# Two parts of a gate's weights loaded into a place of their own, the tied cast reordered, and two parts of a query projection cast early

## The chip, the cores and the metric

One NeuronCore of a Trainium2 chip. The metric is the time of one execution in microseconds (us), the median of several runs. Engines by their short names: PE (TensorE, matmuls), ACT (ScalarE), DVE (VectorE), POOL (GpSimd), SP (SyncE, which here only issues DMAs).

## What is computed

A trunk of two pre-norm layers on 256 tokens of width 1024, float32. Each layer multiplies the normalised input by one wide matrix, splits the result into eleven segments, runs two mixers beside each other (a gated delta rule in both directions, and differential attention), and merges them with two gates:

```python
for l in range(DEPTH):
    h = rmsnorm(x, norm_w[l])
    proj = h @ w_in[l]
    (q_a, k_a, v_a, ab_a, z_a, q_b, k_b, v_b, z_b,
     gate_a, gate_b) = jnp.split(proj, SPLIT_IDX, axis=-1)
    y_a = gated_delta_branch(q_a, k_a, v_a, ab_a, z_a, ...)
    y_b = diff_attention_branch(q_b, k_b, v_b, z_b, ...)
    merged = (sigmoid(gate_a) * (y_a @ w_pa[l])
              + sigmoid(gate_b) * (y_b @ w_pb[l]))
    x = x + merged @ w_out[l]
return rmsnorm(x, final_norm_w)
```

The differential attention has 8 heads, each with two softmaxes over 256 keys whose difference is applied to the values. The delta rule works on chunks of 64 tokens and solves a triangular system for each.

## The kernel before

**Weights in parts.** A projection of 1024 inputs to 1024 outputs is made in two halves of 512 columns, and a half in four parts (kp 0 to 3) of 256 rows. For each part `weights` loads 512 KB (L247, by SP's queue) into a raw tile, casts it to a rounded high part `hi` (L251, on ACT, or on DVE for the parts in `turned`), and takes the rest as a low part, `lo = raw - hi` (L253, on DVE). PE then makes three products of each 128 x 512 block: activation high times hi (L267), high times lo (L268), low times hi (L269); a part is 12 matmuls in `proj_tm`. Raw tiles come from a ring of three ("raw"), hi and lo from rings of two each, so a load can go out when the subtraction that frees its slot is done.

**Homes.** A part can have a home instead of ring tiles for hi and lo: a half of a large tile that is free at the time. Large tiles have tags ("p8" with four buffers, "eo", "ex", "ev", "ktm" and so on), and a new tile of a tag waits for the last reader of the one that had its place. The p8 tiles hold, one after the other, the transposed inputs and the rotated queries and keys of the attention, qkT_0 (heads 0 to 3) and qkT_1 (heads 4 to 7).

**Order of a layer.** The projections follow each other on PE: k and v_b, the first q half, qk (four halves: rotated keys and queries of the attention, named by part and half; qk01 is the second half of the queries), the second q half, v, then zb and za (two halves each), gb, ga (the gates of the attention and of the delta rule), pa and pb, and the output. In layer 0 qk00 starts at 75.8 us, qk01 at 103.4, zb at 163, za at 192, gb at 224.7 and ga at 263. Between them run the decays and the blocks of the triangular solves of the delta rule, on DVE, ACT and POOL, and the attention heads: `scores` (L914, then the maximum L922, the exponentials L924 on ACT, and the combination of the two softmaxes L930 on DVE), `turn` (transposes L941, copy L943) and `attend` (products L952). Head 6's scores come at the end of za's second half, head 7's in gb's first half, and head 7's last products in gb's second half. The solved 32 x 32 blocks are stored to DRAM (udr) and come back in runs of 128 bytes as tiles T (L758, half of them by SP's queue, half by POOL's) and U (L762, POOL's); the products y64p (L776) read T.

**What sets the order.** Each engine runs its instructions in the order of the program, which a list scheduler makes from the source's order, a model of the engines' time, priorities (`high_priority`) and explicit ties (`behind`, which puts an instruction behind another one). Each waits at its place for its inputs. The third and the fourth argument of `gate` give homes to two parts of gb: `wgb` is a pair of p8 tiles, for kp 2 of the first half and kp 1 of the second.

Of the kernel before, what the change touches and what calls it, by code (L numbers as in the profile page):

```python
# [8 lines left out]
F32 = mybir.dt.float32  # L9
F32R = mybir.dt.float32r  # L10
I32 = mybir.dt.int32
AF = mybir.ActivationFunctionType
ALU = mybir.AluOpType
# [4 lines left out]
P = 128  # L18
# [10 lines left out]
HP = None  # L29
# [16 lines left out]
C_QB, C_KB, C_VB, C_ZB, C_GA, C_GB = 4128, 5152, 6176, 7200, 8224, 9248  # L46
# [3 lines left out]
def hybrid_encoder(  # L50
# [18 lines left out]
    nc = tc.nc  # L69
    V, S, G, T = nc.vector, nc.scalar, nc.gpsimd, nc.tensor  # L70
# [6 lines left out]
    wpool = pool("wpool")  # L77
    big = pool("big")
# [25 lines left out]
    mark = {}  # L104
# [116 lines left out]
    def pair(nm):  # L221
        return [big.tile([P, 2, 4, SEQ], F32R, tag="p8", name=f"{nm}_{i}", bufs=4) for i in range(2)]
# [1 line left out]
    def behind(ins):  # L224
        return nullcontext() if ins is None else tc.issue_after(ins)

    def weights(w, c0, n, nm, homes=(None,) * 4, ahead=True, later=None, spare=(), held=None, turned=(), first=()):

        for kp in range(4):
            act, dve = (later or {}).get(kp, (None, None))
            act = mark[nm, act][0] if isinstance(act, int) else act
            with tc.high_priority(offset=HP) if ahead and (homes[kp] is None or kp in first) else nullcontext():
                if homes[kp] is not None:
                    hi, lo = homes[kp] if isinstance(homes[kp], list) else (homes[kp][:, 0], homes[kp][:, 1])
                else:
                    hi = wpool.tile([P, 2, 512], F32R, tag="hi", name=f"hi_{nm}{kp}", bufs=2)
                    lo = wpool.tile([P, 2, 512], F32R, tag="lo", name=f"lo_{nm}{kp}", bufs=2)  # L240
                if kp in spare:
                    raw = work.tile([P, 2, 512], F32, tag="w4a", name=f"raw_{nm}{kp}", bufs=2)
                else:
                    raw = wpool.tile([P, 2, 512], F32, tag="raw", name=f"raw_{nm}{kp}", bufs=3)
                load = (held or {}).get(kp)
                with behind(load):
                    mark["load", nm, kp] = (nc.scalar if load and load.engine != nc.sync.engine else nc.sync).dma_start(  # L247
                        out=raw[:, :, :n],
                        in_=w[kp * 256 : (kp + 1) * 256, c0 : c0 + n].rearrange("(k p) c -> p k c", p=P)).ins
                with behind(act):  # L250
                    high = (V.tensor_copy if kp in turned else S.copy)(hi[:, :, :n], raw[:, :, :n]).ins  # L251
                with behind(dve):
                    mark[nm, kp] = high, V.tensor_tensor(lo[:, :, :n], raw[:, :, :n],  # L253
                                                         hi[:, :, :n].bitcast(F32), ALU.subtract).ins
            for k in range(2):
                yield 2 * kp + k, hi[:, k, :n], lo[:, k, :n]

    def proj_tm(act, w, c0, n, evac, nm, places=(None,) * 4, spare=(), later=None, turned=(), between=None,
                banks=None, held=None, first=()):

        accs = (banks or banks2)(f"pp_{nm}")
        for kt, hi, lo in weights(w, c0, n, nm, places, later=later, spare=spare, turned=turned, held=held,
                                  first=first):
            for m in range(NM):
                ts_ = slice(m * P, (m + 1) * P)
                o = accs[m][:, :n]
                T.matmul(o, act[kt // 4][:, 0, kt % 4, ts_], hi, start=kt == 0, stop=False)  # L267
                T.matmul(o, act[kt // 4][:, 0, kt % 4, ts_], lo, start=False, stop=False)  # L268
                mark["proj"] = T.matmul(o, act[kt // 4][:, 1, kt % 4, ts_], hi, start=False,  # L269
                                        stop=kt == KT - 1).ins  # L270
                mark["done", nm, kt] = mark["proj"]
        if between:
            between()
        for m in range(NM):
            evac(m, accs[m][:, :n])
# [89 lines left out]
    for l in range(DEPTH):  # L365
        lam0 = 0.8 - 0.6 * math.exp(-0.3 * l)
        wl = w_in[l]
# [10 lines left out]
        places = list(homes((("A", 1), ("ktm", 1), ("vtm", 1), ("B", 2)), f"vb{l}"))  # L378
# [4 lines left out]
        later, between, held = {}, None, {}  # L383
# [157 lines left out]
        def conv(seg, c_base, slot, g):  # L541
            def evac_conv(acc, b0):
                vf = []
                for b in range(2):
                    j4 = b0 + b
                    cb = c_base // P + 4 * g + j4
                    ca = work.tile([P, SEQ], F32, tag="conv", name=f"cv{seg}{l}{g}{j4}", bufs=2)
                    S.activation(ca, acc[:, b, :], AF.Copy, scale=cw[:, 2, cb : cb + 1])  # L548
                    for j in (0, 1, 3, 4):
                        sft = j - 2  # L550
                        o0, o1 = max(0, -sft), SEQ - max(0, sft)
                        V.scalar_tensor_tensor(ca[:, o0:o1], acc[:, b, o0 + sft : o1 + sft],  # L552
                                               cw[:, j, cb : cb + 1], ca[:, o0:o1],
                                               ALU.mult, ALU.add)
                    if b == 0:
                        ths = work.tile([P, 2, SEQ], F32, tag="vf", name=f"th{seg}{l}{g}{j4}", bufs=2)
                    th = ths[:, b, :]
                    S.activation(th, ca, AF.Tanh, scale=0.5)
                    if slot is None:
                        f_ = th.rearrange("p (m t) -> p m t", m=NM)  # L560
                    else:
                        f_ = kq[:, 4 * g + j4, :, slot, :]
                    mark["conv"] = V.scalar_tensor_tensor(
                        f_, th.rearrange("p (m t) -> p m t", m=NM), 1.0,
                        ca.rearrange("p (m t) -> p m t", m=NM), ALU.add, ALU.mult).ins
                    vf.append(f_)
                if seg == "q":
                    return
                if seg == "v":
                    tb = squares(f"v{l}{g}{b0}")  # L570
                    turn_squares(tb, ths.rearrange("p b (m t) -> p (b m) t", m=NM))
                    bounce(tb, f"v{l}{g}{b0}")
                    loose.append((tb, 4 * g + b0))
                    return
                pt = bank_c(f"ct{seg}{l}{g}{b0}")
                ptv = pt.rearrange("p (b m d) -> p b m d", b=2, m=NM)
                for b in range(2):
                    for m in range(NM):
                        T.transpose(ptv[:, b, m, :], vf[b][:, m, :], ident)
                bs = slice(4 * g + b0, 4 * g + b0 + 2)  # L580
                S.copy(ktm[:, :, bs, :].rearrange("p m b d -> p b m d"), ptv)
                for b in range(2):
                    for m in range(NM):
                        hd = 4 * g + b0 + b
                        S.activation(sqj[:, :P], ptv[:, b, m, :], AF.Square,
                                     accum_out=ssk[:, m, hd : hd + 1])
            proj_fm(hT, wl, c_base + 512 * g, evac_conv, f"{seg}{l}{g}",
                    turned=(3,) if (seg, g) == ("q", 1) else ())
# [391 lines left out]
            pass  # L980
        log_decays()
        conv("q", C_QA, 1, 0)
        qk_part(0, 0)
        decays(0, 0)
        weigh_k(0, 0)
# [55 lines left out]
                                                   zv[:, j, :], ALU.mult, ALU.mult)  # L1041
                    split_T(yT[i], ov, m, f"{nm}{i}", w=nw_)

        def gate(c_base, nm, tag, between=(None, None), places=((None,) * 4,) * 2, first=()):
            gt = []
            for i in range(2):
                def evac_g(m, ps, i=i):
                    if not gt:
                        gt.extend(e4(nm, tag))
                    S.activation(gt[i][:, m, :], ps, AF.Tanh, scale=0.5)  # L1050
                proj_tm(hT, wl, c_base + 512 * i, 512, evac_g, f"{nm}{i}", places[i], between=between[i],
                        first=first)
            return gt

        def branch(yT, w_, gt, nm, places=(None,) * 4):
            for i in range(2):
# [2 lines left out]
                    V.scalar_tensor_tensor(gs, gs, 1.0, ps, ALU.add, ALU.mult)  # L1059
                proj_tm(yT, w_, 512 * i, 512, evac_p, f"{nm}{i}", (None,) * 4 if i else places)  # L1060

        wgb = [t_.rearrange("p x b t -> p x (b t)").rearrange("p x (k c) -> p x k c", k=2)
               for t_ in pair(f"wgb{l}")]
        gtb = gate(C_GB, f"gb{l}", "ev",
                   (lambda: attend(7, turn(7, es[7], place(34)), place(39)),
                    lambda: [weigh_q(n // 2, n % 2, place((39, 42, 44, 47)[n])) for n in range(4)]),
                   ((None, None, wgb[0], None), (None, wgb[1], None, None)), (1, 2))
        r0 = small.tile([P, NM, NH], F32, tag="r0", name=f"r0{l}")
        V.reciprocal(r0, s_all[:, :, 0, :].rearrange("p h q -> p q h"))
        rb = small.tile([P, NM, NH], F32, tag="rb", name=f"rb{l}")  # L1070
# [126 lines left out]
```

## Time and profile before

| | |
|---|---|
| runs | 768.44, 769.4 and 772.19 us, median 769.4 |
| profiled execution | 770.43 us, span 768.7 us (1.7 us around it) |
| granted clock of PE, mean | 0.996 |
| PE busy | 749.1 us, 97% |
| DVE busy | 577.7 us, 75% |
| ACT busy | 470.8 us, 61% |
| POOL busy | 126.1 us, 16% |
| moved by DMA | 131.24 MB, 171 GB/s |

A row of the timeline gives the start and duration in us, the engine, the line, the operation, what it writes and reads, and in brackets the idle time of the engine before it with what ended it. A row of the windows gives, for a stretch, its length and the busy time (and count) of PE, of PE's weight loads, of DVE, ACT and POOL, then the granted clock of PE, the busy share of the DMA engines and the GB/s. A row of the waits gives the waiting operation, what it waited for, the sum in us, how often, and the longest. Where "x2" stands behind a row, two instructions of a kind came in a row. Durations of PE overlap: a matmul's row runs on after the next has started.

### The profile page before, as it was taken

What the parts mean: (1) busy time and instruction counts of PE and PEld (TensorE: products, weight loads), DVE (VectorE), ACT (ScalarE), POOL (GpSimd) and SP (SyncE); (2) the same over time, 40 slices, a digit from 0 to 9 for tenths busy, and PEclk for the clock granted to TensorE, in tenths of its full rate; (3) what the DMA queues carried; (4) which work ended last, traced back from release to release, by engine and by line L of the source; (5) the groups of instructions that cost most, each with busy time, mean ns of one, the idle gap of its engine ahead of it and who ended that gap; (6) DMA issues with size and microseconds to landing.
All of it is one profiled execution on the core that took longest, in us unless ns stands there. A gap on an engine that the chain in (4) does not pass through costs nothing.

```text
span 768.7 us, 13763 instructions
## 1 busy us (share of the span) xinstructions
PE 749.1 (97%) x5158; PEld 641.8 (83%) x5158; DVE 577.7 (75%) x1083; ACT 470.8 (61%) x1012; POOL 126.1 (16%) x187
## 2 busy tenths in 40 slices
PE   7999999999999999999999999999999889999996
PEld 4899889977877889988889889888787678998884
DVE  5696899999876763478577779999998458437782
ACT  5657675668766574645455668556776557565551
POOL 5100451112031111000010025202111310301000
PEclk9999999999999999999999999999999999999999
DMA  7762767775578242557674257768655934335641
GB/s 230 222 197 60 211 210 210 213 219 171 148 191 202 84 139 86 165 192 239 199 226 140 80 167 245 210 186 232 180 167 160 196 111 133 93 110 192 212 144 55
DMA packets 71795, 131.24 MB, mean 171 GB/s; under 512 B 12288, under 2 KB 12752, under 8 KB 71729
## 3 DMA queue, kind: packets, MB, share of 16 engines
q1 hardware_dynamic: 62718, 111.94, 48.7%
q0 software_dynamic: 6304, 15.15, 7.3%
q10 hardware_dynamic: 2706, 3.28, 1.3%
q8 instruction: 40, 0.66, 0.4%
q14 instruction: 27, 0.21, 0.1%
HBM read 123.44 MB, written 6.91 MB: 170 GB/s over the span
## 4 chain that ended last, share of the span: by engine, by line
PE 72%; DVE 13%; DMA 7%; ACT 4%; issue 3%; POOL 0%; SPq 0%; POOLq 0%; DVEq 0%
PE pp_vb L307 4%; DMA raw_gb<-in_w_in_dram 4%; PE pp_o L307 3%; PE pp_qk L268 2%; PE pp_qk L269 2%; PE pp_qk L267 2%; PE pf_v L323 2%; PE pf_k L327 2%; PE pf_v L327 2%; PE pf_k L325 2%; PE pf_v L325 2%; PE pf_k L323 2%; PE pp_ga L267 2%; PE pp_pb L269 2%; PE pp_ga L269 2%
## 5 line engine op out<-in xcount | busy, mean ns | idle before, releaser
L268 PE MATMUL pp_qk<-lo_qk,hT 128*128 128x512 f32 x128 | 50.9, 398 | 0.2
L269 PE MATMUL pp_qk<-hi_qk,hT 128*128 128x512 f32 x128 | 50.1, 391 | 0.0
L253 DVE TENSOR_TENSOR lo_qk<-raw_qk,hi_qk 128x1024 fp32r<-128x1024 f32 x32 | 40.2, 1257 | 9.7 <-ACT hi_qk L251 9.3
L267 PE MATMUL pp_qk<-hi_qk,hT 128*128 128x512 f32 x128 | 45.2, 393 | 0.0
L251 ACT CAST hi_qk<-raw_qk 128x1024 fp32r<-128x1024 f32 x28 | 29.4, 1050 | 23.5 <-PE pp_qk L269 11.1
L924 ACT ACTIVATE es<-sc,mx 128x256 f32<-128x256 f32 x64 | 29.6, 473 | 17.5 <-DVE mx L922 17.5
L253 DVE TENSOR_TENSOR lo_pb<-raw_pb,hi_pb 128x1024 fp32r<-128x1024 f32 x16 | 19.6, 1225 | 26.8 <-ACT hi_pb L251 26.8
L325 PE MATMUL pf_q<-hT,hi_q 128*128 128x256 f32 x128 | 36.2, 286 | 0.0
L323 PE MATMUL pf_q<-hT,hi_q 128*128 128x256 f32 x128 | 36.1, 287 | 0.0
L323 PE MATMUL pf_v<-hT,hi_v 128*128 128x256 f32 x128 | 35.9, 285 | 0.0
L325 PE MATMUL pf_v<-hT,hi_v 128*128 128x256 f32 x128 | 35.8, 284 | 0.0
L323 PE MATMUL pf_k<-hT,hi_k 128*128 128x256 f32 x128 | 35.7, 284 | 0.0
L325 PE MATMUL pf_k<-hT,hi_k 128*128 128x256 f32 x128 | 35.6, 283 | 0.0
L327 PE MATMUL pf_q<-hT,lo_q 128*128 128x256 f32 x128 | 34.9, 285 | 0.0
L327 PE MATMUL pf_v<-hT,lo_v 128*128 128x256 f32 x128 | 34.5, 288 | 0.0
L327 PE MATMUL pf_k<-hT,lo_k 128*128 128x256 f32 x128 | 34.4, 284 | 0.0
L552 DVE SCALAR_TENSOR_TENSOR cvq<-pf_q,cw,cvq 128x254 f32<-128x254 f32 (+1 forms) x64 | 29.9, 476 | 1.9 <-ACT cvq L548 1.4
L251 ACT CAST hi_pa<-raw_pa 128x1024 fp32r<-128x1024 f32 x16 | 16.9, 1055 | 22.2 <-PE pp_pa L269 16.0
L552 DVE SCALAR_TENSOR_TENSOR cvv<-pf_v,cw,cvv 128x254 f32<-128x254 f32 (+1 forms) x64 | 30.0, 477 | 0.1
L268 PEld LDWEIGHTS pp_qk<-lo_qk,hT 128*128 128x128 f32 x128 | 24.0, 188 | 7.2 <-DVE lo_qk L253 2.3
L552 DVE SCALAR_TENSOR_TENSOR cvk<-pf_k,cw,cvk 128x254 f32<-128x254 f32 (+1 forms) x64 | 28.5, 478 | 2.0 <-ACT cvk L548 1.3
L269 PEld LDWEIGHTS pp_qk<-hi_qk,hT 128*128 128x128 f32 x128 | 24.0, 188 | 4.9
(370 smaller groups left out, 2522.4 us busy)
## 6 DMA issues: line engine op xcount, KB each, us to landing
raw_qk<-in_w_in_dram SPq DMA_DIRECT2D x32, 512.0 KB, 3.8
raw_k<-in_w_in_dram SPq DMA_DIRECT2D x16, 512.0 KB, 4.9
raw_q<-in_w_in_dram SPq DMA_DIRECT2D x16, 512.0 KB, 3.7
raw_v<-in_w_in_dram SPq DMA_DIRECT2D x16, 512.0 KB, 3.8
raw_zb<-in_w_in_dram SPq DMA_DIRECT2D x16, 512.0 KB, 3.7
raw_za<-in_w_in_dram SPq DMA_DIRECT2D x16, 512.0 KB, 3.8
raw_gb<-in_w_in_dram SPq DMA_DIRECT2D x16, 512.0 KB, 5.6
raw_ga<-in_w_in_dram SPq DMA_DIRECT2D x16, 512.0 KB, 4.0
```

What stands on the lines that cost most here:

```text
L251: high = (V.tensor_copy if kp in turned else S.copy)(hi[:, :, :n], raw[:, :, :n]).ins
L253: mark[nm, kp] = high, V.tensor_tensor(lo[:, :, :n], raw[:, :, :n], hi[:, :, :n].bitcast(F32), ALU.subtract).ins
L267: T.matmul(o, act[kt // 4][:, 0, kt % 4, ts_], hi, start=kt == 0, stop=False)
L268: T.matmul(o, act[kt // 4][:, 0, kt % 4, ts_], lo, start=False, stop=False)
L269: mark["proj"] = T.matmul(o, act[kt // 4][:, 1, kt % 4, ts_], hi, start=False, stop=kt == KT - 1).ins
L307: mark["proj"] = T.matmul(o, a_, w_, start=kt == 0 and a_ is ah and w_ is hi, stop=kt == KT - 1 and a_ is al).ins
L323: T.matmul(o, hi[:, cs], act[kt // 4][:, 0, kt % 4, :], start=first, stop=False, skip_group_check=True)
L325: T.matmul(o, hi[:, cs], act[kt // 4][:, 1, kt % 4, :], start=False, stop=False, skip_group_check=True)
L327: T.matmul(o, lo[:, cs], act[kt // 4][:, 0, kt % 4, :], start=False, stop=done, skip_group_check=True)
L552: V.scalar_tensor_tensor(ca[:, o0:o1], acc[:, b, o0 + sft : o1 + sft], cw[:, j, cb : cb + 1], ca[:, o0:o1], ALU.mult, ALU.add)
L924: S.activation(es[:, n, qt, :], spv[:, qt, :], AF.Exp, bias=mx[:, n, qt : qt + 1], accum_out=s_all[:, h, n, qt : qt + 1])
```

## The change

Three edits. First, gb's parts 2 and 3 of the first half are no longer loaded into the ring: one p8 tile, `rgb`, holds the raw weights of both, and their hi and lo come from the rings. Second, only kp 1 of the second half has a home for its hi and lo (`wgb`, now one tile), and its cast is tied behind the cast of kp 0 of that half (`later`). Third, `cast_ahead` loads and casts kp 0 and 1 of qk01 ahead of qk00, with hi and lo in tiles of the tags "eo" and "ex"; `weights` then finds them in `ready`.

```diff
-    def weights(w, c0, n, nm, homes=(None,) * 4, ahead=True, later=None, spare=(), held=None, turned=(), first=()):
+    def weights(w, c0, n, nm, homes=(None,) * 4, ahead=True, later=None, spare=(), held=None, turned=(), first=(), raws={}):
...
         for kp in range(4):
+            if (nm, kp) in ready:
+                hi, lo = ready.pop((nm, kp))
+                for k in range(2):
+                    yield 2 * kp + k, hi[:, k, :n], lo[:, k, :n]
+                continue
...
-                if kp in spare:
+                if kp in raws:
+                    raw = raws[kp]
+                elif kp in spare:
...
+    def cast_ahead(w, c0, nm, kp, tag):
+
+        hi, lo = (big.tile([P, 2, 512], F32R, tag=tag, name=f"{x_}_{nm}{kp}", bufs=2) for x_ in ("ah", "al"))
+        raw = wpool.tile([P, 2, 512], F32, tag="raw", name=f"raw_{nm}{kp}", bufs=3)
+        with tc.high_priority(offset=HP):
+            nc.sync.dma_start(out=raw, in_=w[kp * 256 : (kp + 1) * 256, c0 : c0 + 512].rearrange("(k p) c -> p k c", p=P))
+            high = S.copy(hi, raw).ins
+            mark[nm, kp] = high, V.tensor_tensor(lo, raw, hi.bitcast(F32), ALU.subtract).ins
+        ready[nm, kp] = hi, lo
...
         log_decays()
         conv("q", C_QA, 1, 0)
+        for kp, tag in enumerate(("eo", "ex")):
+            cast_ahead(wl, C_QB + 512, f"qk{l}01", kp, tag)
         qk_part(0, 0)
...
                 proj_tm(hT, wl, c_base + 512 * i, 512, evac_g, f"{nm}{i}", places[i], between=between[i],
-                        first=first)
+                        later={1: (0, None)} if i and places[i][1] is not None else None,
+                        first=first, raws=raws[i])
...
-        wgb = [t_.rearrange("p x b t -> p x (b t)").rearrange("p x (k c) -> p x k c", k=2)
-               for t_ in pair(f"wgb{l}")]
+        rgb = big.tile([P, 2, 2, 512], F32, tag="p8", name=f"rgb{l}", bufs=4)
+        wgb = big.tile([P, 2, 2, 512], F32R, tag="p8", name=f"wgb{l}", bufs=4)
...
-                   ((None, None, wgb[0], None), (None, wgb[1], None, None)), (1, 2))
+                   ((None,) * 4, (None, wgb, None, None)), (1,),
+                   ({2: rgb[:, 0], 3: rgb[:, 1]}, {}))
```

How the order of the engines' programs moves, in layer 0 (layer 1 is alike). A name's number tells apart tiles of one name. SP's queue before, from the last za loads on: raw_gb_2645, 2663, 2679 and 2697 are the four parts of gb's first half, 2736, 2752, 2770 and 2788 those of the second.

```order
L247 DMA raw_za_2498<-in_w_in_dram 128x2x512
L247 DMA raw_za_2516<-in_w_in_dram 128x2x512
L247 DMA raw_gb_2645<-in_w_in_dram 128x2x512
L247 DMA raw_gb_2663<-in_w_in_dram 128x2x512
L247 DMA raw_gb_2679<-in_w_in_dram 128x2x512
L247 DMA raw_gb_2697<-in_w_in_dram 128x2x512
L758 DMA T_2628<-udr_343 32x16x32 x2
L247 DMA raw_gb_2736<-in_w_in_dram 128x2x512
L758 DMA T_2628<-udr_343 32x16x32 x2
L247 DMA raw_gb_2752<-in_w_in_dram 128x2x512
L247 DMA raw_gb_2770<-in_w_in_dram 128x2x512
```

And now, first at the head of za's second half, then from gb's part 0 on (raw_gb_2645 and 2663 stand just ahead of the second piece).

```order
L254 DMA raw_za_2360<-in_w_in_dram 128x2x512
L254 DMA rgb_2639<-in_w_in_dram 128x2x512 x2
L254 DMA raw_za_2462<-in_w_in_dram 128x2x512
...
L254 DMA raw_gb_2736<-in_w_in_dram 128x2x512
L254 DMA raw_gb_2752<-in_w_in_dram 128x2x512
L777 DMA T_2628<-udr_343 32x16x32 x4
L254 DMA raw_gb_2770<-in_w_in_dram 128x2x512
```

The loads of kp 2 and 3 of the first half went to the front, into rgb, and the first two loads of the second half stand ahead of the four T loads instead of among and behind them.

ACT before, from the cast of gb's part 0 to that of the second half's part 0 (es_2543 belongs to head 6, es_2577 to head 7).

```order
L251 CAST hi_gb_2643<-raw_gb_2645 128x1024
L943 COPY aT_2537<-at_2536 128x512
L251 CAST wgb_0_2639<-raw_gb_2679 128x1024
L924 ACTIVATE es_2543,s_all_350<-sc_2546,mx_2544 128x256 x2
...
L251 CAST hi_gb_2695<-raw_gb_2697 128x1024
L943 COPY aT_2571<-at_2570 128x512
L924 ACTIVATE es_2577,s_all_350<-sc_2580,mx_2578 128x256 x2
L924 ACTIVATE es_2577,s_all_350<-sc_2579,mx_2578 128x256 x2
L251 CAST wgb_1_2640<-raw_gb_2752 128x1024
L251 CAST hi_gb_2734<-raw_gb_2736 128x1024
```

And now, in the same stretch (hi_gb_2679 and hi_gb_2696 are cast from rgb).

```order
L962 COPY aT_2537<-at_2536 128x512
L943 ACTIVATE es_2543,s_all_350<-sc_2546,mx_2544 128x256 x2
L943 ACTIVATE es_2543,s_all_350<-sc_2545,mx_2544 128x256 x2
L258 CAST hi_gb_2643<-raw_gb_2645 128x1024
...
L943 ACTIVATE es_2577,s_all_350<-sc_2580,mx_2578 128x256 x2
L943 ACTIVATE es_2577,s_all_350<-sc_2579,mx_2578 128x256 x2
L258 CAST hi_gb_2679<-rgb_2639 128x1024
...
L258 CAST hi_gb_2696<-rgb_2639 128x1024
L962 COPY aT_2714<-at_2713 128x512
L258 CAST hi_gb_2734<-raw_gb_2736 128x1024
L258 CAST wgb_2640<-raw_gb_2752 128x1024
```

The cast into wgb_0 ahead of head 6's exponentials is gone, part 0's cast stands behind them, and the cast into wgb stands behind that of hi_gb_2734.

PE before, at the end of gb's first half.

```order
L268 MATMUL pp_gb_2642<-lo_gb_2696,hT_1_108 128x512
L269 MATMUL pp_gb_2642<-hi_gb_2695,hT_1_108 128x512
L267 MATMUL pp_gb_2732<-hi_gb_2734,hT_0_107 128x512
L267 MATMUL pp_gb_2733<-hi_gb_2734,hT_0_107 128x512
L268 MATMUL pp_gb_2732<-lo_gb_2735,hT_0_107 128x512
L269 MATMUL pp_gb_2732<-hi_gb_2734,hT_0_107 128x512
...
L654 MATMUL kq_2804<-kq_329 128x128
L776 MATMUL y64p_3191<-T_2621,A_339 32x32
L776 MATMUL y64p_3226<-T_2628,A_339 32x32
```

And now, at the same place (y64p comes 64 times between the two pieces).

```order
L288 MATMUL pp_gb_2642<-hi_gb_2696,hT_1_108 128x512
L971 MATMUL av_2720<-vb_1_133,aT_2714 128x128
L673 MATMUL kq_2804<-kq_329 128x128
L971 MATMUL av_2720<-vb_1_133,aT_2714 128x128
L673 MATMUL kq_2804<-kq_329 128x128
...
L795 MATMUL y64p_3226<-T_2628,A_339 32x32
L286 MATMUL pp_gb_2732<-hi_gb_2734,hT_0_107 128x512
```

Head 7's products (av_2720), the first products kq of the decays, and all y64p now stand ahead of gb's second half; before, they stood behind its part 1.

DVE before, where the parts of qk01 are cast (hi_qk_1327 and 1345 are its kp 0 and 1, 1363 its kp 2; kk are products of the decays' blocks).

```order
L680 TENSOR_TENSOR A_339<-kk_1081,dsum_1079 128x512
L251 CAST hi_qk_1327<-raw_qk_1329 128x1024
L253 TENSOR_TENSOR lo_qk_1328<-raw_qk_1329,hi_qk_1327 128x1024
L679 TENSOR_TENSOR dsum_1103<-B_340 128x512
L251 CAST hi_qk_1345<-raw_qk_1347 128x1024
L680 TENSOR_TENSOR A_339<-kk_1105,dsum_1103 128x512
L253 TENSOR_TENSOR lo_qk_1346<-raw_qk_1347,hi_qk_1345 128x1024
L679 TENSOR_TENSOR dsum_1127<-B_340 128x512
```

And now, first among the convolutions of the second k half (cvk), then at the place of before.

```order
L571 SCALAR_TENSOR_TENSOR cvk_656<-pf_k_534,cw_268,cvk_656 128x254
L274 TENSOR_TENSOR al_qk_964<-raw_qk_965,ah_qk_963 128x1024
L582 SCALAR_TENSOR_TENSOR kq_329<-thk_513,cvk_516 128x2x128
...
L571 SCALAR_TENSOR_TENSOR cvk_683<-pf_k_535,cw_268,cvk_683 128x255
L274 TENSOR_TENSOR al_qk_970<-raw_qk_971,ah_qk_969 128x1024
L571 SCALAR_TENSOR_TENSOR cvk_683<-pf_k_535,cw_268,cvk_683 128x254
...
L260 TENSOR_TENSOR lo_q_1273<-raw_q_1274,hi_q_1272 128x1024
L260 TENSOR_TENSOR lo_qk_1364<-raw_qk_1365,hi_qk_1363 128x1024
L698 TENSOR_TENSOR dsum_1091<-B_340 128x512
L699 TENSOR_TENSOR A_339<-kk_1093,dsum_1091 128x512
L698 TENSOR_TENSOR dsum_1115<-B_340 128x512
```

The two casts and two subtractions of kp 0 and 1 are gone from between the blocks; two subtractions (al_qk) stand among the convolutions, and the two casts are on ACT.

More of the change, by code (lines that the diff above doesn't have):

```diff
@@ L256, in weights @@
                 yield 2 * kp + k, hi[:, k, :n], lo[:, k, :n]
+    ready = {}
+    def cast_ahead(w, c0, nm, kp, tag):
[6 more added lines that the diff above has]
+        ready[nm, kp] = hi, lo
     def proj_tm(act, w, c0, n, evac, nm, places=(None,) * 4, spare=(), later=None, turned=(), between=None,
[L259 removed]
+                banks=None, held=None, first=(), raws={}):
         accs = (banks or banks2)(f"pp_{nm}")
         for kt, hi, lo in weights(w, c0, n, nm, places, later=later, spare=spare, turned=turned, held=held,
[L263 removed]
+                                  first=first, raws=raws):
             for m in range(NM):
@@ L1042, in gated, with gate @@
                     split_T(yT[i], ov, m, f"{nm}{i}", w=nw_)
-        def gate(c_base, nm, tag, between=(None, None), places=((None,) * 4,) * 2, first=()):
+        def gate(c_base, nm, tag, between=(None, None), places=((None,) * 4,) * 2, first=(),
+                 raws=({}, {})):
             gt = []
```

## The prediction

> **What bounds the kernel now.** I read the busy shares first, then PE's waits over the whole span, then the 20 us windows in which PE falls short, and last the timeline of each engine in those windows.
>
> ```profile
> PE 749.1 (97%) x5158; PEld 641.8 (83%) x5158; DVE 577.7 (75%) x1083; ACT 470.8 (61%) x1012; POOL 126.1 (16%) x187
> PE at L941 <- DVE es L930: 2.8, 2, 1.6
> PE pp_gb L267 <- ACT hi_gb L251: 2.7, 2, 2.3
> PE pp_gb L268 <- DVE lo_gb L253: 1.4, 2, 0.7
> 220.00:240.00 20.00, 18.41 (x100) 14.52 (x99) 11.14 (x20) 10.80 (x30) 6.90 (x12) 1.00 0.91 228
> 600.00:620.00 20.00, 15.85 (x75) 11.92 (x74) 11.26 (x19) 13.27 (x37) 5.13 (x10) 0.96 0.80 160
> 60.00:200.00 140.00, 139.78 (x856) 121.09 (x855) 127.28 (x262) 95.46 (x217) 31.52 (x47) 1.00 0.64 187
> ```
>
> PE is busy 97% of the span, so only time in which PE stands still, or runs at a lower clock, can be won. Three lines of its waits, 6.9 us in all, belong to one place that comes twice: the projection gb of each layer (about 224 to 248 us and 597 to 624 us). The windows say the same: 18.41 and 15.85 of 20 us there, against 139.78 of 140 between the start and z.
>
> The timeline of PE in layer 1 (start, duration, idle time before in brackets) shows three stops; "x2" is two matmuls in a row.
>
> ```profile
> 600.82 0.39 PE L269 MATMUL pp_gb<-hi_gb,hT 128*128 128x512 f32 x1
> 602.38 0.74 PE L941 MATMUL at<-ident,es 128*128 128x128 f32 x4 [1.17 <-DVE es L930]
> 613.33 0.39 PE L268 MATMUL pp_gb<-lo_gb,hT 128*128 128x512 f32 x1
> 613.55 0.39 PE L269 MATMUL pp_gb<-hi_gb,hT 128*128 128x512 f32 x1
> 616.20 0.73 PE L267 MATMUL pp_gb<-hi_gb,hT 128*128 128x512 f32 x2 [2.26 <-ACT hi_gb L251]
> 617.65 0.50 PE L268 MATMUL pp_gb<-lo_gb,hT 128*128 128x512 f32 x1 [0.72 <-DVE lo_gb L253]
> ```
>
> Matmuls of this shape start 0.22 to 0.23 us apart when nothing stops them (613.33 to 613.55); a stop costs the distance of the starts less 0.23. At 602.38 that is 1.56 - 0.23 = 1.33 us; at 616.20 it is 2.65 - 0.23 = 2.42; the second matmul of the pair starts 0.73 - 0.39 = 0.34 after 616.20, so the stop at 617.65 costs 1.11 - 0.23 = 0.88. Sum 4.6 us. Layer 0 has the same three:
>
> ```profile
> 228.06 0.39 PE L269 MATMUL pp_gb<-hi_gb,hT 128*128 128x512 f32 x1
> 230.04 0.74 PE L941 MATMUL at<-ident,es 128*128 128x128 f32 x4 [1.59 <-DVE es L930]
> 241.21 0.39 PE L269 MATMUL pp_gb<-hi_gb,hT 128*128 128x512 f32 x1
> 241.99 0.73 PE L267 MATMUL pp_gb<-hi_gb,hT 128*128 128x512 f32 x2 [0.40 <-ACT hi_gb L251]
> 243.44 0.50 PE L268 MATMUL pp_gb<-lo_gb,hT 128*128 128x512 f32 x1 [0.72 <-DVE lo_gb L253]
> ```
>
> 1.98 - 0.23 = 1.75, 0.78 - 0.23 = 0.55, and 1.11 - 0.23 = 0.88: 3.2 us. After the long stop of layer 1 the granted clock drops as well:
>
> ```profile
> 618.00:620.00 2.00, 2.00 (x7) 1.61 (x6) 0.78 (x1) 1.69 (x3) 0.00 (x0) 0.63 0.88 302
> 620.00:622.00 2.00, 2.00 (x6) 1.53 (x5) 0.45 (x1) 0.40 (x1) 0.00 (x0) 0.52 0.78 222
> ```
>
> The clock is the last number but two: 0.63 and 0.52 in those 4 us, so 2 x (0.37 + 0.48) = 1.7 us of full-speed work are missing. Together 3.2 + 4.6 + 1.7 = **9.5 us** lie in the two gb stages.
>
> **Why PE stops there.** ACT takes its work in order, and two of its casts wait for a load:
>
> ```profile
> 226.24 1.05 ACT L251 CAST wgb<-raw_gb 128x1024 fp32r<-128x1024 f32 x1 [4.34 <-DMA raw_gb<-in_w_in_dram]
> 239.94 1.05 ACT L251 CAST wgb<-raw_gb 128x1024 fp32r<-128x1024 f32 x1 [3.01 <-DMA raw_gb<-in_w_in_dram]
> 598.58 1.05 ACT L251 CAST wgb<-raw_gb 128x1024 fp32r<-128x1024 f32 x1 [3.92 <-DMA raw_gb<-in_w_in_dram]
> 614.15 1.04 ACT L251 CAST wgb<-raw_gb 128x1024 fp32r<-128x1024 f32 x1 [4.88 <-DMA raw_gb<-in_w_in_dram]
> 615.11 1.04 ACT L251 CAST hi_gb<-raw_gb 128x1024 fp32r<-128x1024 f32 x1
> DMA to landing us min/median/max: 3.6/5.6/9.7
> 220.28 2.79 SPq L247 DMA_DIRECT2D raw_gb<-in_w_in_dram  x2
> 228.58 0.39 SPq L247 DMA_DIRECT2D raw_gb<-in_w_in_dram  x1
> 232.05 10.60 SPq L247 DMA_DIRECT2D raw_gb<-in_w_in_dram  x3
> 604.39 12.46 SPq L247 DMA_DIRECT2D raw_gb<-in_w_in_dram  x3
> ```
>
> The first wgb cast (598.58) stands ahead of the exponentials of head 6; they start when it is done, DVE's es L930 follows, and PE's transposes at L941 wait for that. The second (614.15) waits for a load issued at 604.39 and landed at 614.13, and stands ahead of the cast of the part that PE needs first (615.11): a cast that is needed later holds up one that is needed now.
>
> **The change, part by part.** (1) Parts 2 and 3 of gb's first half are loaded straight into a large tile of their own before z's second half. The two loads that stood at 220.28 are no longer there, and the first two loads of the second half move up into their place, ahead of the T loads: from 228.58 and 232.05 to about 220.3 and 223 (the slots of the ring come free as before). With the longest landing of any gb load, 9.7 us, they are in by 230 and 233, and PE wants the first at about 241. In ACT's order no cast of gb stands ahead of head 6's exponentials any more; the cast into wgb comes after that of part 0 of its half. So both waits on a load go: -1.75 and -1.33 (transposes), -0.55 and -2.42 (hi), -0.88 twice (lo). What is late next on the transposes' path is the chain mx, es, L930; the trace's windows from 60 to 200, where the same heads run with no cast waiting, lose 0.2 us in 140, so it fits. The lower clock follows the longest stop within 2.5 us, and I take it to go with it: -1.7. **Sum -9.5**, bounds 0 (all stops stay) and -9.5.
>
> Beside that place, the Trainium skill, page "TensorE: Matmul & The Clock Gate", section "Why this matters for your kernels", asks for no PE-idle gap over about 3 us, since one idle window halves the clock. Here a gap of 2.65 us with a second of 1.1 us behind it already halved it, and the 1.98 us gap of layer 0 did not; the measurement decides. By the page's figure alone the half clock would have another cause than this gap and would stay, and the sum would be -7.8.
>
> (2) The two loads into the large tile must wait for the last reader of the tile whose room they take, the scores of head 3, and za's second half queues behind them on SP.
>
> ```profile
> 181.68 25.18 SPq L247 DMA_DIRECT2D raw_za<-in_w_in_dram  x8
> 196.85 1.13 PE L914 MATMUL sc<-qkT 64*128 64x256 f32 x8
> ```
>
> In the new order these scores stand ahead of za's first part on PE; now they stand behind a few matmuls of it, and end at 198. The eight za loads go out some 3.5 us apart (25.18 over seven steps), the fifth at about 196. So even at the scores' old place it would go some 2 us later, and no wait of PE for za is among those above 0.2 us: the loads run ahead of need. Cost 0, bounds 0 and 2 a layer.
>
> (3) Two parts of qk's second q projection (kp 0 and 1) are cast early: two loads, two ACT casts and two DVE subtractions a layer move from about 100 us to about 55 to 67 us.
>
> ```profile
> 100.00:120.00 20.00, 19.86 (x119) 16.79 (x118) 19.65 (x33) 12.89 (x31) 9.90 (x14) 1.00 0.73 212
> 60.00:80.00 20.00, 20.00 (x140) 18.67 (x139) 13.62 (x30) 15.07 (x45) 2.93 (x1) 1.00 0.30 82
> L253 DVE TENSOR_TENSOR lo_qk<-raw_qk,hi_qk 128x1024 fp32r<-128x1024 f32 x32 | 40.2, 1257 | 9.7 <-ACT hi_qk L251 9.3
> 100.78 0.68 DVE L251 CAST hi_qk<-raw_qk 128x1024 fp32r<-128x1024 f32 x1
> 101.56 1.61 DVE L253 TENSOR_TENSOR lo_qk<-raw_qk,hi_qk 128x1024 fp32r<-128x1024 f32 x1
> ```
>
> DVE is full at 100 to 120 us (19.65) and has room at 60 to 80 (13.62). It loses 2 x (0.68 + 1.61) = 4.6 us there and takes 2 x 1.26 = 2.5 us on here; ACT takes 2 x 1.05 on, with 5 us free. On the path that sets the end this is worth only PE's idle time of those stretches, 0.14 us in this window and 0.1 in that of layer 1: **-0.3**, bounds 0 and -1.
>
> (4) What these pieces push back. In layer 0 the logarithms of the decays, and what follows from them down to the solves, come behind the new pieces on ACT and DVE: 0 to 2 x (1.05 + 1.26) = 4.6 us later. qk's own first parts are cast on the same two engines right after, and could reach PE late by as much. I take 1 us of new stops in all, near the end at 0, since DVE has 6 us free in 60 to 80: **+1.0**, bounds 0 and 4.6. With the casts out of the way, the order also places head 7's last product and the first solve products (y64p) ahead of gb's second half on PE. These need the T loads:
>
> ```profile
> L758 POOL DMA_DIRECT2D T<-udr x4: 648/648/649, 230.3 to 232.3; - x4
> DMA to landing us min/median/max: 2.2/5.9/7.9
> 235.76 1.05 PE L952 MATMUL av<-vb,aT 128*128 128x128 f32 x8
> ```
>
> The last issue at 232.3 plus the longest landing 7.9 is 240.2; PE comes there at about 241.44 - 1.75 + 1.6 (eight products of head 7 and eight of the solve, some 0.8 us for each eight: 1.05 less the 0.25 by which the last one's duration runs on) = 241.3. Slack 1 us, and two big loads fewer are in flight beside them. Cost 0, with the price in a rival.
>
> **Sum.** The profiled execution took 770.43 us (span 768.7): 770.4 - 9.5 - 0.3 + 1.0 = 761.6. It lies 1.0 over the median of 769.4, so on the median **760.6 us**.
>
> **Rivals.** A difference under 0.5% (3.8 us) can't be told from none.
> - A, as above: 760.6; 758 to 763.5. Chance 0.56.
> - B, the wait moves on: T lands 1 to 3 us later than reckoned, or the solves' inputs are late by (4), and PE, which now meets y64p ahead of a projection part that could have covered it, stands 0 to 2 us in each layer; or the lower clock stays (1.7). For it: DMA was 0.91 busy in 220 to 240. Against: the same issue times and less traffic. 760.6 + 2 to 5 = 763 to 765.5. Chance 0.22.
> - C, the change doesn't do what it says: loads ahead on SP get no earlier, since the ring's slots come free later, behind the casts that now stand behind the exponentials on ACT. Then the hi and lo stops (1.43 and 3.30) and the clock stay, and only the transposes' 3.1 go: 769.4 - 3.1 - 0.3 + 1 = 767. Against: the ring has two users fewer. Chance 0.14.
> - D, slower: y64p's T waits on the whole decay chain of (4), in both layers. A chain 4.6 us later leaves PE 3.6 us at y64p in each, 7.2 in all, which takes the gain to 768; from 6 us later in each layer (5 us of stop, 10 in all, over the 9.8 gained) the kernel is slower, and at 8 us (14 of stop) it takes 773.6. For it: that order puts the decays behind two more casts. Against: the decays are made over 100 us ahead of T's loads, and DVE has idle time on the way to take a delay up. Chance 0.08.
>
> **How the numbers follow.** The likeliest is A. From 757.5 (A with (4) at 0, the 1.0 of (3), and 1 us between runs) to 767.5 (up to C) lie some 8 in 10. Faster by over 0.5% is below 765.6: A and nearly all of B, 0.77. Within: C and a rest of D and B, 0.17. Slower: 0.06.
>
> **What would show it.** Right: no wait of ACT on a gb load, PE's waits at L941 and at the gb matmuls under 0.3 us each, PE at least 19.7 of 20 in 220 to 240 and in the same stretch of layer 1, and the granted clock at 1.00 there. For B and D: a PE wait at y64p on T or U. For C: the casts of gb's second half still waiting for a landing. For (4): waits of PE on lo_qk between 75 and 90 us. Wrong outright: a new stop in ga, pa or pb, whose order I read as hardly changed.

## The result, and the profile after

The changed kernel takes 766.95 us (median of 20 runs, 765.16 to 769.83), the kernel before 769.47 (median of 20). The ratio is 0.9969, with a 95% interval of 0.9954 to 0.9984: 2.4 us faster, by 1.2 to 3.5. The forecast was 760.6, or 8.8 us less than the median of before. The profiled execution took 765.96 us (span 764.3), 4.5 less than that of before; single executions lie up to 4 us from their median, so the medians carry the size, and the profiles the places.

The page of the changed kernel, its busy line:

```profile
PE 746.6 (98%) x5158; PEld 640.3 (84%) x5158; DVE 572.3 (75%) x1079; ACT 475.3 (62%) x1016; POOL 122.7 (16%) x187
```

PE's idle time fell from 19.6 to 17.7 us, 1.9, where 6.9 had been at gb alone. What PE waits for now, without the layers' first projection (operation, releaser, sum in us, times, longest):

```profile
PE wb_n L165 <- POOL tri L116: 3.1, 1, 3.1
PE pp_zb L287 <- DVE lo_zb L260: 2.6, 3, 1.6
PE pf_q L346 <- DVE lo_q L260: 1.4, 2, 0.7
PE at L960 <- DVE es L949: 0.6, 1, 0.6
PE pp_pa L287 <- DVE lo_pa L260: 0.5, 1, 0.5
```

The three gb lines of before are gone altogether; the wait at L960 (L941 before) that is left is one in za. In their place stand lines that the list of before does not have: the low parts of zb, of the first q half (lo_q) and of pa. The windows at gb, in both layers (length, then busy time of PE; the clock is the last number but two):

```profile
220.00:240.00 20.00, 20.00 (x106) 16.20 (x107) 13.99 (x24) 14.05 (x38) 9.28 (x16) 1.00 0.97 211
594.00:614.00 20.00, 20.00 (x109) 16.14 (x108) 13.62 (x22) 15.22 (x39) 7.01 (x13) 1.00 0.80 178
552.00:556.00 4.00, 2.37 (x13) 1.73 (x12) 4.00 (x8) 3.60 (x11) 0.56 (x1) 1.00 0.26 74
```

PE never stops in the first two, and the granted clock is 1.00 in all three. The last row is the new hole: in zb of layer 1, PE stands 1.63 of 4 us.

PE's timeline at the new stops:

```profile
70.80 0.39 PE L346 MATMUL pf_q<-hT,lo_q 128*128 128x256 f32 x1 [0.67 <-DVE lo_q L260]
183.23 0.50 PE L287 MATMUL pp_zb<-lo_zb,hT 128*128 128x512 f32 x1 [0.85 <-DVE lo_zb L260]
554.57 0.50 PE L287 MATMUL pp_zb<-lo_zb,hT 128*128 128x512 f32 x1 [1.63 <-DVE lo_zb L260]
567.01 0.41 PE L960 MATMUL at<-ident,es 128*128 128x128 f32 x2 [0.63 <-DVE es L949]
```

Counted from start to start, as in the prediction, the stops of the trace are: lo_q 0.83 and 0.86, lo_zb 1.02 in layer 0 and 0.33 + 1.79 in layer 1, the transposes 0.79, lo_pa 0.69. Sum 6.3 us, against the 9.5 us (7.8 of stops, 1.7 of lower clock) that left gb. The question for the experiments was which edit brought the 6.3, and by what.

### The profile page after: what moved, and what is told of

Its sections match the earlier page's. It is cut to its first block, busy times and chain, and to the rows that moved or that the text cites. A ratio compares the mean times of both kernels' runs of the same rounds, so it can differ in the third digit from the quotient of the medians.

```text
span 764.3 us, 13758 instructions
## 1 busy us (share of the span) xinstructions
PE 746.6 (98%) x5158; PEld 640.3 (84%) x5158; DVE 572.3 (75%) x1079; ACT 475.3 (62%) x1016; POOL 122.7 (16%) x187
## 5 line engine op out<-in xcount | busy, mean ns | idle before, releaser
L287 PE MATMUL pp_qk<-lo_qk,hT 128*128 128x512 f32 x112 | 43.9, 392 | 0.0
L288 PE MATMUL pp_qk<-hi_qk,hT 128*128 128x512 f32 x112 | 43.7, 390 | 0.0
L260 DVE TENSOR_TENSOR lo_qk<-raw_qk,hi_qk 128x1024 fp32r<-128x1024 f32 x28 | 34.4, 1228 | 9.0 <-ACT hi_qk L258 8.8
L286 PE MATMUL pp_qk<-hi_qk,hT 128*128 128x512 f32 x112 | 39.7, 392 | 0.0
L260 DVE TENSOR_TENSOR lo_pb<-raw_pb,hi_pb 128x1024 fp32r<-128x1024 f32 x16 | 19.6, 1226 | 23.0 <-ACT hi_pb L258 23.0
L260 DVE TENSOR_TENSOR lo_ga<-raw_ga,hi_ga 128x1024 fp32r<-128x1024 f32 x16 | 19.5, 1219 | 20.6 <-ACT hi_ga L258 20.6
L287 PE MATMUL pp_zb<-lo_zb,hT 128*128 128x512 f32 x64 | 26.0, 407 | 2.6 <-DVE lo_zb L260 2.6
```

## The experiments

**Two theories.** O: the gb edit is worth its whole gain, and the two parts cast ahead cost about 6 us by the stops above. G: the gb edit is worth only part, because what fills its stops comes late elsewhere, and the parts cast ahead are harmless. Each run is compared with runs of the kernel before on the same chip.

**1. The gb edit alone.**

```diff
-        for kp, tag in enumerate(("eo", "ex")):
-            cast_ahead(wl, C_QB + 512, f"qk{l}01", kp, tag)
```

> The change without the two parts cast ahead; gb's raw tile and the tied cast stay. Theory O (the two parts cast ahead cost about 6 us by the stops that appear at lo_q, at lo_zb, at the transposes in za and at lo_pa; the gb edit is worth its whole 9.5): 760 us, ratio to before 0.987 to 0.989, no PE wait over 0.3 us between 60 and 224 us. Rival G (the stops of gb are only partly won, since what fills them comes late elsewhere, and the parts cast ahead are harmless): 766 to 767, with stops in z as in the changed kernel.

Measured 761.29 us (ratio 0.9908, 0.9882 to 0.9934), 1.3 above the 760 of theory O and far from G. Of PE's waits, outside the layers' first steps there is left:

```profile
PE pp_pa L287 <- DVE lo_pa L260: 0.5, 1, 0.5
```

No gb, no z, no q line. lo_pa is new against the kernel before, so that stop belongs to the gb edit.

**2. The two parts cast ahead alone**, gb as in the kernel before (homes, order and loads of before, `cast_ahead` kept).

> The kernel before with only the two parts of qk01 cast ahead; gb as before. Theory O: slower, 773 to 776 us (before + 4 to 6.5), with the waits of PE at lo_q (0.8 a layer), at lo_zb (1.0 in layer 0, 2.1 in layer 1) and at the transposes in za, and gb's stops as before. Rival G: 769 to 770, no difference.

Measured 774.81 us (ratio 1.0085, 1.006 to 1.011): 6.7 us slower.

```profile
PE pp_zb L287 <- DVE lo_zb L260: 3.6, 3, 1.9
PE pp_gb L286 <- ACT hi_gb L258: 2.9, 2, 2.6
PE at L960 <- DVE es L949: 2.3, 2, 1.7
PE pf_q L346 <- DVE lo_q L260: 1.8, 2, 1.0
```

Here both families stand together: gb's old stops and the new ones. Runs 1 and 2 decide for O: the gb edit wins 6.9 us and the early parts cost 6.7. The whole change gave -2.4 and the sum of the two is -0.2; each part is uncertain by about 2 us, so it is not shown whether they add.

**3. One part (kp 0) instead of two.** The loop is `enumerate(("eo",))`.

> The change with one part (kp 0) of qk01 cast ahead instead of two. The order of the engines' programs in the stages zb and za is then that of the kernel before again, while the order up to qk01 is changed. Theory O, with the order in z as the cause of the larger half (3.9 of 6.3 us): 760 to 762 us, no stop at lo_zb and at the transposes. If instead the added work itself is the cause (one part is half of it): 763 to 764, with stops in z of half the size. Rival G: 766 to 767.

Measured 759.73 us (0.9885, 0.9862 to 0.9909), with none of the new stops but lo_pa (0.5 again), and one in k of layer 1 (abq) that runs 1 and 2 don't have:

```profile
PE abq L526 <- ACT abT L523: 1.3, 1, 1.3
```

Half of the added work costs none of the 6 us. It is not the amount of work alone, then. In this kernel the order of PE, ACT and DVE in zb and za is that of before, row for row; in the changed kernel it is another one, in both layers, on all three engines.

**4. The same work, the other order.** One part again, but kp 2. That leaves the q halves nearly as before, and gives z, in both layers, the order of the changed kernel's layer 0.

> As the run with one part cast ahead, but kp 2 of qk01 instead of kp 0: the same added work (one load, one ACT cast, one DVE subtraction a layer). The programs' order in the first and second q half is then nearly that of the kernel before, and in zb and za, in both layers, that of layer 0 of the changed kernel. If the order in z is the cause of its stops: a stop of PE at lo_zb of about 1 us in each layer, 761.5 to 763 us. If the amount of work cast ahead is the cause: none, 759.5 to 760.5 us, as with kp 0.

Measured 763.1 us (0.9923, 0.9899 to 0.9948), with stops at lo_zb in both layers (0.66 and 0.86 from start to start) and none at lo_q (besides lo_pa, 0.7 us at abq and 0.2 at lo_qk are left):

```profile
PE pp_zb L287 <- DVE lo_zb L260: 1.2, 2, 0.7
```

**5. Two parts, z's order as before.** kp 1 and 2 in layer 0, kp 0 in layer 1.

> Two parts (kp 1 and 2) of qk01 cast ahead in layer 0, one (kp 0) in layer 1: the order in zb and za is that of the kernel before in both layers, while layer 0's order in the q halves is changed as in the changed kernel. If the order in z is the cause: no stop at lo_zb or at the transposes; a stop at lo_q of up to 0.9 us in layer 0 alone; 759.7 to 761 us. If the work of two parts is the cause: a stop of about 1 us at lo_zb in layer 0 as in the changed kernel, 761.5 to 763 us.

Measured 761.13 us (0.9896, 0.9873 to 0.9919). PE waits for lo_q, once, in the layer with two parts; no wait for lo_zb:

```profile
PE pf_q L346 <- DVE lo_q L260: 0.8, 1, 0.8
```

**6. Two parts in both layers, z's order as before only in layer 0** (kp 1 and 2 there, kp 0 and 1 in layer 1).

> Two parts cast ahead in both layers: kp 1 and 2 in layer 0, where the order in z is that of the kernel before, and kp 0 and 1 in layer 1, where it is that of the changed kernel's layer 1. If the order in z is the cause: no stop in z in layer 0, and in layer 1 the 2.1 us at lo_zb and 0.8 at the transposes; with 0.8 us at lo_q in each layer 763.5 to 765 us. If the work is the cause: stops in z in both layers, 766 to 767 us.

Measured 766.31 us (0.9966, 0.995 to 0.9982). By the time alone this is the 766 to 767 us of the other theory, in which the work is the cause; the profiled execution took 764.87 and was the fastest of the twelve. The places decide, and they are those of the order: lo_q in both layers (1.6 us of waits), lo_zb at 536.87 and 553.10, in layer 1 alone, and the transposes at 565.60. Why the median lies 1.3 us over the 763.5 to 765 expected is open.

Runs 3 to 6 cross work and order: the stops in z follow the order, and the stop at lo_q follows two parts in a layer.

**7. What in the order does it.** ACT in zb of layer 1; first the changed kernel, then the one before:

```profile
548.86 0.70 ACT L618 ACTIVATE vtm<-tb_v,nrm 128x128 f32<-128x128 f32 x2 [1.24 <-DMA tb_v<-bnc_v]
549.46 0.40 ACT L577 ACTIVATE thv<-cvv 128x256 f32<-128x256 f32 x1
549.77 0.68 ACT L618 ACTIVATE vtm<-tb_v,nrm 128x128 f32<-128x128 f32 x2
550.36 0.58 ACT L355 ACTIVATE zb<-pp_zb 128x512 f32<-128x512 f32 x1
550.83 1.04 ACT L258 CAST hi_zb<-raw_zb 128x1024 fp32r<-128x1024 f32 x1
```

```profile
549.43 0.61 ACT L336 ACTIVATE zb<-pp_zb 128x512 f32<-128x512 f32 x1
549.90 1.07 ACT L251 CAST hi_zb<-raw_zb 128x1024 fp32r<-128x1024 f32 x1
550.84 0.63 ACT L336 ACTIVATE zb<-pp_zb 128x512 f32<-128x512 f32 x1
551.33 1.30 ACT L599 ACTIVATE vtm<-tb_v,nrm 128x128 f32<-128x128 f32 x4
```

The copies vtm bring the values of the delta rule back from a turn through DRAM (tb_v). Before, they stood behind the cast of zb's second half, kp 1; now they stand ahead of it, and ACT waits 1.24 us for their DMA. ACT's wait of this kind adds up to

```profile
ACT vtm L618 <- DMA tb_v<-bnc_v: 6.3, 4, 2.8
```

in the changed kernel. Where z has no stops, the list of ACT's waits has no such line (before and run 5), or one of 0.8 and 0.3 us (runs 1 and 3); in runs 2, 4 and 6 it has 9.4, 3.7 and 3.4 us.

How the wait reaches PE is seen on DVE, in the changed kernel (the last row is PE in run 6):

```profile
177.76 0.42 DVE L582 SCALAR_TENSOR_TENSOR thv<-thv,cvv 128x256 f32<-128x256 f32 x1 [1.09 <-ACT thv L577]
181.96 1.21 DVE L260 TENSOR_TENSOR lo_zb<-raw_zb,hi_zb 128x1024 fp32r<-128x1024 f32 x1
549.90 0.42 DVE L582 SCALAR_TENSOR_TENSOR thv<-thv,cvv 128x256 f32<-128x256 f32 x1 [0.46 <-ACT thv L577]
553.30 1.22 DVE L260 TENSOR_TENSOR lo_zb<-raw_zb,hi_zb 128x1024 fp32r<-128x1024 f32 x1
564.73 0.17 DVE L946 RECIPROCAL cc<-s_all 128x2 f32<-128x2 f32 x1 [2.19 <-ACT es L943]
553.10 0.50 PE L287 MATMUL pp_zb<-lo_zb,hT 128*128 128x512 f32 x1 [1.06 <-DVE lo_zb L260]
```

It does not come by the cast: that ends at 551.87, and DVE takes up lo_zb at 553.30. It comes by thv, a step of the convolution that stands behind the first of the copies on ACT, and for which DVE stands idle. In layer 0 DVE loses 1.09 us there and has no gap from there to lo_zb, and PE stops for 1.02. In layer 0 of run 2 and both layers of run 4, with the same order, DVE loses 1.78, 0.70 and 0.90 us there, and PE's stops are 1.71, 0.66 and 0.86: this stop is the wait for tb_v. The transposes hang on it as well, by the exponentials behind the fourth batch of copies (ACT waits 2.75 us for it, DVE 2.19).

In layer 1 it is the smaller part: DVE loses 0.46 us, and PE stops for 1.79. In run 6, with that order in layer 1, DVE loses nothing on the way to lo_zb and PE still stops for 1.22. The rest is the order on DVE itself: between the subtractions of kp 0 and kp 1 DVE works 4.71 us in the kernel before (548.51 to 553.22) and 5.79 in run 6 (546.04 to 551.83). The 0.33 at the first stop has no wait for tb_v ahead of it either. So of the 3.9 us in z, 2.3 (1.02, 0.46 and 0.79) hang on tb_v and 1.7 (0.33 and 1.33) on DVE's order, as worked out from these rows.

To test the wait for tb_v, the copies alone were tied to where they stood, with the rest of the change whole:

```diff
                 place_v(mark[f"zb{l}0", 1][0])
-                place_v(mark[f"zb{l}0", 3][0])
             elif p == 1:
                 place_v(mark[f"zb{l}1", 1][0])
+            elif p == 2:
+                place_v(mark[f"za{l}0", 1][0])
```

> The whole change, with two batches of the copies vtm on ACT tied later: the third behind zb's second half, kp 1, the fourth behind za's first half, kp 1, which is where they stand in the kernel before. The order in the q halves (with its stops at lo_q) and from ga on stays that of the changed kernel. Theory: in the changed kernel these copies came ahead of that cast of zb and ACT stood waiting for their DMA (tb_v), 1.2 to 2.8 us, which made lo_zb and the transposes late. Then the stops at lo_zb (3.1 us in all) and at the transposes (0.8) go and those at lo_q (1.7) stay: 763 to 764 us, ratio to before 0.991 to 0.993. If the stops in z come from DVE's own crowding and not from that wait: 766 to 767.5 us.

Measured 762.7 us (0.9916, 0.9894 to 0.9937). The line on tb_v is gone from ACT's waits; of PE's, past the layers' start:

```profile
PE pf_q L346 <- DVE lo_q L260: 1.7, 2, 0.8
PE pp_pa L287 <- DVE lo_pa L260: 0.5, 1, 0.5
PE pp_zb L287 <- DVE lo_zb L260: 0.3, 2, 0.2
```

The waits for lo_zb fall from 2.6 to 0.3 us, those at the transposes go, and lo_q stays (1.7), at 0.3 us under the time expected. But the tie also put DVE's rows in z in another order than either kernel: the two subtractions of layer 1 are 4.87 us apart (546.61 to 551.48), near the 4.71 of before. So this run takes both causes away at once and does not tell them apart; the rows above do.

**8. The stop at lo_q.** The first q half's kp 2, DVE in the changed kernel:

```profile
64.67 1.23 DVE L274 TENSOR_TENSOR al_qk<-raw_qk,ah_qk 128x1024 fp32r<-128x1024 f32 x1 [0.56 <-ACT ah_qk L273]
65.81 0.48 DVE L571 SCALAR_TENSOR_TENSOR cvk<-pf_k,cw,cvk 128x254 f32<-128x254 f32 x1
66.21 0.41 DVE L582 SCALAR_TENSOR_TENSOR kq<-thk,cvk 128x256 f32<-128x256 f32 x1
67.72 0.43 DVE L582 SCALAR_TENSOR_TENSOR kq<-thk,cvk 128x256 f32<-128x256 f32 x1 [1.10 <-ACT thk L577]
68.09 1.52 DVE L571 SCALAR_TENSOR_TENSOR cvk<-pf_k,cw,cvk 128x254 f32<-128x254 f32 x3
69.53 1.22 DVE L260 TENSOR_TENSOR lo_q<-raw_q,hi_q 128x1024 fp32r<-128x1024 f32 x1
```

lo_q's cast begins at 67.95 on ACT and takes 1.04, so it is ready at 68.99; DVE is still at the three convolution steps of 68.09, which the early part pushed back, and starts 0.54 us later than it could. The early part pushes on two engines: its subtraction takes 1.23 us of DVE, and its cast stands on ACT ahead of its load, and ahead of the thk that DVE waits 1.10 us for:

```profile
63.59 1.05 ACT L273 CAST ah_qk<-raw_qk 128x1024 fp32r<-128x1024 f32 x1 [1.59 <-DMA raw_qk<-in_w_in_dram]
```

To test it, the two subtractions were tied behind those of q's parts 2 and 3:

```diff
+            with behind(mark[f"q{nm[2]}0", 2 + kp][1]):
-            mark[nm, kp] = high, V.tensor_tensor(lo, raw, hi.bitcast(F32), ALU.subtract).ins
+                mark[nm, kp] = high, V.tensor_tensor(lo, raw, hi.bitcast(F32), ALU.subtract).ins
```

> The change, with the two early subtractions tied behind the subtractions of the first q half's parts 2 and 3. The stop at lo_q (0.83 and 0.86) comes from the early subtractions standing ahead of lo_q on DVE: with the tie it goes, in both layers. The order in z is now that of the changed kernel's layer 1 in both layers: 2.9 us of stops in each, so 766 to 768 us in all (0.83 + 0.86 less, 1.9 more in layer 0). If the stop at lo_q has another cause (the loads, or ACT), it stays and the time is 768 to 769.

Measured 775.27 us (1.0089, 1.006 to 1.0119).

```profile
PE pf_v L343 <- ACT stg L487: 3.1, 2, 1.6
PE pp_zb L288 <- DVE lo_zb L260: 2.6, 2, 1.5
PE av L972 <- ACT aT L963: 2.4, 2, 1.7
```

The wait at lo_q is gone, but the time was missed by 7 us: the tie moved qk and v as well (pf_v waits 3.1 us for ACT's stg, which stood nowhere in the list), and ACT waits 9.6 us for tb_v. It moved the second early cast on ACT, too, from 63.59 to 74.21, behind the first q casts. So the stop goes when the second early part leaves the stretch ahead of lo_q, as in runs 3 and 4; whether its subtraction or its cast's wait does more is not told apart. The tie is no cure.

**9. The halves of the gb edit.** The tie without the raw tile, put into the kernel before:

```diff
+                        later={1: (0, None)} if i and places[i][1] is not None else None,
```

> The kernel before with only the cast of gb's second half, kp 1, tied behind that of kp 0; loads and homes as before. The hi and lo stops at gb's second half (0.55 and 0.88 in layer 0, 2.42 and 0.88 in layer 1) go, and if the lower clock comes from the long stop its 1.7 us too; the stops at the transposes (1.75 and 1.33) stay: 769.5 - 4.7 - 1.7 = 763, ratio 0.991 to 0.993. If the lower clock has another cause it stays: 764.8. If the part that now comes second is late in its turn: 767 to 769.

Measured 765.74 us (0.9965, 0.9948 to 0.9982), less gain than the 6.4 expected. The hi and lo stops of gb's second half are gone, but the other stop grew:

```profile
PE at L941 <- DVE es L930: 4.3, 2, 2.4
```

ACT's cast ahead of it, in layer 0, and two windows behind it, one in each layer (the clock is the last number but two):

```profile
225.66 1.05 ACT L251 CAST wgb<-raw_gb 128x1024 fp32r<-128x1024 f32 x1 [5.14 <-DMA raw_gb<-in_w_in_dram]
```

```profile
232.00:234.00 2.00, 2.00 (x6) 1.56 (x5) 1.48 (x3) 1.00 (x2) 0.69 (x3) 0.50 1.42 151
604.00:606.00 2.00, 2.00 (x9) 1.18 (x8) 1.48 (x3) 1.97 (x6) 1.61 (x4) 0.50 1.09 247
```

The wait at the transposes is 4.3 us against 2.8 before, and the clock is down to 0.50 after it in both layers. PE came to it at 226.64, 1.4 us earlier than in the profile of before, but the load that ACT waits for landed only 0.6 us earlier: here the wait for the load took back more than half of what was won ahead of it.

The raw tile without the tie (and without the parts cast ahead):

> The gb edit without the tie and without the parts cast ahead: two raw parts in a tile of their own, the cast into wgb where the scheduler puts it, now ahead of head 7's exponentials on ACT. If the raw tile, which lets the loads of gb's second half go out 8 us earlier, does the work alone: wgb's load has landed when its cast comes up, no stop, 760 to 762 us as with the tie. If the tie is needed: ACT waits at the wgb cast for its load, the transposes of head 7 or the products behind them are late by 1 to 2.5 us in each layer, 763 to 766 us.

Measured 761.78 us (0.9906, 0.9885 to 0.9927), no gb line among PE's waits, and none of ACT on a gb load: the tile for the raw parts does it alone, and the tie adds nothing that shows (0.9906 against run 1's 0.9908).

## Why the prediction was wrong, point by point

- **(1), -9.5 at gb: right.** All six stops and the lower clock are gone. The gb edit alone wins 6.9 us by the medians, with an interval of 5.1 to 9.1 (0.66 to 1.18% of 768.15); 9.5 less the 0.7 that lo_pa takes back, 8.8, lies inside, near its end. The 1.7 of the clock is read from one execution: the mean clock of the kernel before runs from 0.991 to 0.999 over its executions, that of run 1 from 0.996 to 0.998. Of the signs, ACT still waits for a gb load once, 1.5 us at 616.91, which PE doesn't feel.
- **(2), the wait of the loads into the raw tile: right, no cost.** No wait of PE for za came with that tile. The products y64p did not wait either, so rivals B and D had the wrong place, and the loads did land earlier, so C did not happen; that C's figure was 767, next to the 766.95 measured, is luck. D's own sums don't agree: its 768 has the 1.0 of (4) in it, its 773.6 has not.
- **(3), -0.3 for the early parts: the sign held, by one part.** With one part the median is 759.73, against 761.29 without any, on the same chip; their ranges (759.13 to 761.12, 760.26 to 762.88) overlap, so it is likely, not shown.
- **(4), +1.0 for what the pieces push back: this is the step that failed.** It measured 5.6 us: lo_q 1.7, lo_zb 3.1, the transposes 0.8. The prediction's words "I take 1 us of new stops in all, near the end at 0, since DVE has 6 us free in 60 to 80" argue from DVE's share over 20 us, and the cost was looked for between 75 and 90 us, at lo_qk. The stop came at 70 us, where DVE was half a microsecond behind at one place, though it stands free for 4.6 of the 20 us there; and not all of the ACT time that (3) counts as free was free, since ACT waits 6.7 us in all for the early parts' own loads. The larger part, 3.9 us, came over 110 us later, where nothing of the early parts is left: the sum has no term for z, and takes the programs' order there as that of before, though it had changed with the edit. The order at gb and at qk01 was read; in z, where DVE is busy 20.00 of 20 us in the kernel before (160 to 180 and 540 to 560), it was not. Such an order has two costs here: copies ahead of their DMA, 2.3 us, and more work of DVE ahead of a subtraction that PE needs, 1.7.
- **A sign of being wrong that came: a new stop in pa.** PE waits 0.5 us for lo_pa at 717.02 (0.7 from start to start). The raw tile without the tie and without early parts has it too, so it comes with that tile; what makes lo_pa late stays open.
- **The size of the range:** 766.95 lies at the top of 757.5 to 767.5, but as a gain it is 2.4 us against 8.8 forecast.

## What to carry to other kernels

When a scheduler lays out the order, an edit can move what stands ahead of a wait in a stage that it does not touch. Compare the order of every stage in which an engine is full, and look for an instruction with a DMA behind it that has come ahead of a cast on an engine that works in order: here it was the same fault at gb (a cast ahead of its load), at lo_q (an early cast ahead of its load) and in z (copies ahead of tb_v). Look as well at how much work has come in front of an instruction that PE waits for: in z that was 1.7 of the 3.9 us. A version with one part ahead, 759.7 us, and one with the v copies tied, 762.7, both beat the kernel before and the changed one.

## What the runs showed of the hardware that was not expected

The granted clock fell to one half after gaps of PE, from start to start, of 2.65 us (before), 3.01 (run 2, at gb), 2.82 and 2.28 us (run 9, tie only), and stayed at 1.00 after 2.32 us (run 2, 558.93 to 561.25):

```profile
562.00:564.00 2.00, 2.00 (x10) 1.60 (x10) 2.00 (x5) 0.40 (x2) 1.07 (x2) 1.00 0.79 215
```

So the length of the gap does not decide alone. In these four places the half clock lasts 3.41 us, and in all twelve profiles each fall lies a whole number of 3.413 us after the clock's first rise (before: 604.16 us, 177 times). Cut on that grid, first the kernel before around its fall, and last the changed kernel's idlest stretch:

```profile
615.10:618.51 3.41, 1.60 (x6) 1.03 (x7) 2.36 (x2) 3.35 (x10) 0.00 (x0) 1.00 0.25 42
618.51:621.92 3.41, 3.41 (x10) 2.63 (x9) 1.23 (x1) 1.50 (x3) 0.00 (x0) 0.50 0.88 281
552.37:555.78 3.41, 1.78 (x9) 1.18 (x8) 3.41 (x8) 3.23 (x10) 0.56 (x1) 1.00 0.28 83
```

In the stretch ahead of each of the four falls PE is busy 1.60 us (before), 1.26 (run 2), 1.55 and 1.52 (run 9). From the first rise to the last fall of the twelve profiles, every stretch of the grid with 1.60 us of work or less has a fall behind it, and none with the last row's 1.78 or more. In these runs the clock falls, then, when PE is idle for about half of a stretch or more: a gap of 2.28 us inside one stretch did it (run 9, layer 1), and one of 2.32 us that the grid cut in two did not (run 2).

The Trainium skill, page "TensorE: Matmul & The Clock Gate", section "What's actually happening", has the clock halved after an idle window of about 3.4 us that runs freely. The length and the free running agree with these traces; a window idle as a whole does not, since 1.60 us of work in it did not keep the clock up, and the measurement decides.
